# Attention value products of both weight parts in one 256-wide matmul, in a hybrid encoder block

## Chip, core and metric

The kernel runs on one core of one Trainium2 chip. The metric is the device time of one execution in microseconds (us). The kernel before has a median of 2099.49 us in three runs (2098.23 to 2099.73).

## Reference

One layer of an encoder in fp32 on 1024 tokens (16 rows of 64 columns) of width 1024. The change lies in the mixer, between the two feed-forward halves:

```python
u = rms_norm(h); q, k, v, s_in, gates = jnp.split(u @ w_in, splits, axis=-1)
# 8 heads of 64; a query sees min(8, rows) x 16 tokens around it, clamped at the grid's edge
sc = q . k * 64 ** -0.5 + bias          # in the window
pr = softmax(sc, axis=-1)
y_attn = (pr . v) @ w_attn_out
y_ssm = s5_branch(s_in, ...) @ w_ssm_out   # two-directional state scan, D skip, GLU
g_attn, g_ssm = sigmoid(gates)
h = h + (g_attn * y_attn + g_ssm * y_ssm) @ w_out
```

Before it stands `h + swiglu(rms_norm(h)) / 2`; behind it another such half, a small per-layer embedding with a gate, and a last norm.

## The kernel before

**Number format.** TensorE (PE) reads fp32 values that are split in two: a high part, which ScalarE (ACT) rounds into the format that PE takes (`split`, L152 to L154, a CAST), and a low part, the rest, which VectorE (DVE) subtracts out. A product of two split operands is three matmuls (`mm3`, L182 to L186: high by high, high by low, low by high), most of them 512 wide.

**Order of work.** The order of PE's instructions is the order of the code, written by hand. DVE, ACT, GpSimd (POOL) and SyncE (SP, which issues most loads) are put in order by a scheduler when the kernel is built, but for the start and `end()` (L1678), whose DVE and ACT order is the code's too. An engine runs its instructions strictly in that order. Tiles come out of rings of a fixed number of buffers: a writer waits until the last reader of the buffer's earlier content is done. The rings that matter: `x`, 56 buffers of 128 x 512 (`thid` and `tx`); in the mixer `w`, 12 of 128 x 1024 (`tw`: weights split in high and low, keys, and so on); `st`, 3 of 128 x 1024 for raw loads; `tmp`, 4 of 128 x 512; and 8 banks of PSUM (`bank`).

**Stages.** First feed-forward half to about 700 us, mixer to about 1255 us, its output product, second feed-forward half, embedding, last norm to 2094.5 us. In the mixer PE works through projections of `u` (24 matmuls, 512 wide, per output tile of 128 x 512: q, k, v, the state branch's input, 16 gate tiles). A generator, `mixer_side` (L1286), runs beside it: `tick()` after each three matmuls of a projection counts down, and when the count is up the next piece of the generator is issued in the middle of the projection. So the attention and the state branch are small insertions between 512-wide matmuls.

**Attention** comes in 64 units j: 8 heads, 2 row halves, 4 column blocks. A unit has 128 queries and 12 x 24 or 12 x 32 keys. At iteration j of the generator (one each 4 ticks, each 3 ticks from j = 48):

- `attn_scores` (L1198): two matmuls, 288 or 384 wide (L1207, L1208), then bias, maximum, exponential and division on DVE and ACT; the weights stay in `sm`.
- `attn_turn` (L1219) for unit j - 3: three transposes by PE (L1223) into a bank `pt`, split by ACT (L1226) into `pth` and by DVE (L1227) into `ptl`.
- `attn_values` (L1230) for unit j - 5: the values `vhl` of 64 dimensions lie high beside low, 128 columns. For each of three key groups one matmul of `pth`, 128 wide, with all 128 columns as weights (L1235: rows 0 to 63 get v_high x p_high, rows 64 to 127 v_low x p_high), and one of `ptl` with the 64 high columns (L1237, added to rows 0 to 63). A bank `O` collects four column blocks; after the fourth ACT copies the lower rows out (L1241), DVE adds them to the upper rows and brings the columns into token order (L1242), and a DMA from ACT's queue stores 64 x 512 in `o_d` (L1245).
- two steps of the state scan on POOL (L1092 to L1094, tile `X`), 128 steps in all; at j = 48 all that are left.

From j = 48 each iteration also takes one of 16 pairs of state groups: `ssm_out` (L1097) loads coefficients (`emi`), copies the pair's states out of `X` into `xs` by two ACT and two DVE copies (L1111), and three iterations later PE forms `yo` from them (L1117, L1119); ACT copies `yo` out (L1121).

After the units comes the state branch's GLU. Then `load_br` (L1400) loads both branches, the attention from `o_d` as two loads of 128 x 1024 per row half, and splits them into `bh` and `bl` for the products `br`.

Of the kernel before, what the change touches and what calls it, by code (L numbers as in the profile page):

```python
# [8 lines left out]
F32 = mybir.dt.float32  # L9
# [7 lines left out]
P = 128  # L17
SEQ = 1024
HT = 512
# [19 lines left out]
def encoder_block(ctx, tc, I, out):  # L39
# [73 lines left out]
    a2_d = dtile("a2_d", [NF // 2, 7, P, HT])  # L113
    h2_d = dtile("h2_d", [P, NK * SEQ])
    v_d = dtile("v_d", [SEQ, 512])
    o_d = dtile("o_d", [512, SEQ])
    g_d = dtile("g_d", [16, P, SEQ])
    y_d = dtile("y_d", [NPD, P, NCH])
    y2_d = dtile("y2_d", [512, SEQ])
# [81 lines left out]

        return tc.issue_after(mark["ins"]) if "ins" in mark else nullcontext()

    def rstd(m, r, q):
        A.activation(r, m, AF.Abs_reciprocal_sqrt, bias=eps)
        V.tensor_tensor(q, r, r, ALU.mult)
        V.scalar_tensor_tensor(q, m, eps, q, ALU.add, ALU.mult)
        V.scalar_tensor_tensor(r, q, -3.0, r, ALU.add, ALU.mult)

    class Norm:  # L210
# [33 lines left out]
        def stat(self, r=None, summed=False):  # L244
            if summed:
                m = self.acc
            else:
                m = bank("ms")[:, 0:self.n]
                sums = [self.acc] + self.more
                for i, sq in enumerate(sums):  # L250
                    T.matmul(m, lhsT=ones, rhs=sq, start=i == 0, stop=i == len(sums) - 1)
            q = tmq("rq", [P, self.n])
            r = thid("rs", [P, self.n], F32) if r is None else r
            rstd(m, r, q)
            self.r = r

        def apply(self, gi, res, every):
# [839 lines left out]
    def ssm_out(pr):  # L1097

        ms = []
        for g in range(2):  # L1100
            em = thid("emi", [P, 4, NCH], F32)
            nc.sync.dma_start(em[:, 0:3].rearrange("p a b -> p (a b)"), e_d[2 * pr + g])
            nc.sync.dma_start(em[:, 3], u_d[2 * pr + g])
            ms.append(em)

        xs = tw("xs", [P, 2, 2, NCH], F32)
        for g in range(2):
            for r in range(2):
                s0 = Xv[g * 64:(g + 1) * 64, r, pr, 0:1]
                both = bass.AP(tensor=s0.tensor, offset=s0.offset, ap=[list(s0.ap[0]), [NCH + 2, 2], [1, NCH]])  # L1110
                (A.copy if g == r else V.tensor_copy)(xs[r * 64:(r + 1) * 64, g], both)  # L1111

        def go():
            o = bank("yo")
            for g in range(2):
                oo = o[:, g * NCH:(g + 1) * NCH]
                T.matmul(oo, lhsT=ms[g][:, 0], rhs=ms[g][:, 3], start=True, stop=False)  # L1117
                for d in range(2):
                    T.matmul(oo, lhsT=ms[g][:, 1 + d], rhs=xs[:, g, d], start=False, stop=(d == 1))  # L1119
            ys = tmp("ys", [P, 2, NCH])  # L1120
            A.copy(ys, o[:, 0:2 * NCH].rearrange("p (g c) -> p g c", g=2))  # L1121
            nc.scalar.dma_start(y_d[2 * pr:2 * pr + 2].rearrange("g p c -> p g c"), ys)
        return go
# [10 lines left out]
    def qk_proj(hp, wq, wk):  # L1134
        qs, kh, kl = [], [], []
        for t in range(2):
            o = proj(wq, t, "q")
            for i in range(2):
                if t == 0:
                    qs.append(tw("qs"))  # L1140
                src = o[i * 64:(i + 1) * 64].rearrange("p (r b c) -> p r b c", r=8, b=4)
                hs, ls = slice(i * 64, (i + 1) * 64), slice((1 - i) * 64, (2 - i) * 64)

                def view(sl):
                    return qs[i][sl, hsl(t)].rearrange("p (b r c) -> p r b c", b=4, r=8)
                A.copy(view(hs), src)
                V.tensor_tensor(view(ls), src, view(hs).bitcast(F32), ALU.subtract)
        for t in range(2):
            o = proj(wk, t, "k")
            for i in range(2):  # L1150
                if t == 0:
                    kh.append(tw("kh"))
                    kl.append(tw("kl"))
                hs, ls = slice(i * 64, (i + 1) * 64), slice((1 - i) * 64, (2 - i) * 64)
                A.activation(kh[i][hs, hsl(t)], o[hs], AF.Copy, scale=0.125)
                A.activation(kh[i][ls, hsl(t)], o[hs], AF.Copy, scale=0.125)
                for s_ in (hs, ls):
                    V.scalar_tensor_tensor(kl[i][s_, hsl(t)], o[hs], 0.125, kh[i][hs, hsl(t)].bitcast(F32),
                                           ALU.mult, ALU.subtract)
        for i in range(2):  # L1160
            qkv[2 * hp + i] = (qs[i], kh[i], kl[i])

    def load_v(hd, cb):
        n = 4 * KNC[cb]
# [33 lines left out]
    def attn_scores(hd, rb, cb):  # L1198
        q, kh, kl = qkv[hd]
        n = KNC[cb]  # L1200
        nk = 12 * n
        qv = q[:, rb * HT + cb * P:rb * HT + (cb + 1) * P]
# [4 lines left out]
        T.matmul(s3, lhsT=qv, rhs=kv(kh), start=True, stop=False)  # L1207
        T.matmul(s3, lhsT=qv, rhs=kv(kl), start=False, stop=True)  # L1208
        sm = thid("sm", [P, 384], F32)[:, 0:nk]
        st = ap_.tile([P, 4], F32, tag="stat", bufs=4, name="stat")  # L1210
        V.tensor_tensor_reduce(out=sm.rearrange("p (r c) -> p r c", c=n), in0=s3,
                               in1=tabs[hd, rb][KVAR[cb]][:, :, 0:n], scale=-1.0, scalar=3.0e38,
                               op0=ALU.add, op1=ALU.min, accum_out=st[:, 0:1])
        A.activation(sm, sm, AF.Exp, bias=st[:, 0:1], scale=-1.0, accum_out=st[:, 1:2])
        V.reciprocal(st[:, 2:3], st[:, 1:2])
        A.activation(sm, sm, AF.Copy, scale=st[:, 2:3])
        return sm

    def attn_turn(cb, sm):  # L1219
        kp = 4 * KNC[cb]  # L1220
        tp = bank("pt")
        for g in range(3):
            T.transpose(tp[0:kp, ksl(g)], sm[:, g * kp:(g + 1) * kp], ident)  # L1223
# [6 lines left out]
    def attn_values(hd, rb, cb, O, ph, pl):  # L1230
        kp = 4 * KNC[cb]
        hl = vld[hd, cb]
        for g in range(3):

            T.matmul(O[:, ksl(cb)], lhsT=hl[0:kp, rb + g].rearrange("p h d -> p (h d)"), rhs=ph[0:kp, ksl(g)], start=(g == 0), stop=False,  # L1235
                     skip_group_check=True)
            T.matmul(O[0:64, ksl(cb)], lhsT=hl[0:kp, rb + g, 0], rhs=pl[0:kp, ksl(g)], start=False, stop=(g == 2),  # L1237
                     skip_group_check=True)
        if cb == 3:
            ot, ol = tmp("ot"), tmp("ol")  # L1240
            A.copy(ol[0:64], O[64:128])  # L1241
            V.tensor_tensor(ot[0:64].rearrange("p (r b c) -> p b r c", r=8, b=4),  # L1242
                            O[0:64].rearrange("p (b r c) -> p b r c", b=4, r=8),
                            ol[0:64].rearrange("p (b r c) -> p b r c", b=4, r=8), ALU.add)
            nc.scalar.dma_start(o_d[hd * 64:(hd + 1) * 64, hsl(rb)], ot[0:64])  # L1245


    ydr = y_d.rearrange("g (t o) c -> g o t c", o=16)
# [37 lines left out]
    def mixer_side():  # L1286
# [31 lines left out]
        for j in range(n + 6):  # L1318
            if j < n:
# [3 lines left out]
                if cb == 0 and j > 0:  # L1323
                    make_tabs(hd, rb)
                sms[j] = attn_scores(hd, rb, cb)
            if 0 <= j - 3 < n:
                pts[j - 3] = attn_turn(units[j - 3][2], sms.pop(j - 3))
            if 0 <= j - 5 < n:
                hd, rb, cb = units[j - 5]
                if cb == 0:  # L1330
                    O[hd, rb] = bank("O")
                attn_values(hd, rb, cb, O[hd, rb], *pts.pop(j - 5))
                if rb == 1 and hd + 1 < NH:
                    load_v(hd + 1, cb)
            scan_steps(2)
            if j >= SO:
                p = j - SO
# [62 lines left out]
    def load_br(t, b):  # L1400

        res = []
        if b == 0:
            for k in range(0, 4, 2):
                st = tst("br")
                nc.sync.dma_start(st.rearrange("p (k c) -> p k c", k=2),
                                  o_d[k * P:(k + 2) * P, hsl(t)].rearrange("(k p) c -> p k c", p=P))
                for i in range(2):
                    hi, lo = tx("bh"), tx("bl")
                    split(hi, lo, st[:, hsl(i)])  # L1410
                    res.append((hi, lo))
            return res
        for k in range(4):
# [264 lines left out]
    def end():  # L1678
# [131 lines left out]
```

## Time and profile before

| | before |
|---|---|
| median of 3 runs | 2099.49 us (2098.23 to 2099.73) |
| the profiled execution's time | 2096.29 us |
| its span in the profile | 2094.5 us |
| granted TensorE clock | 0.998 |
| busy: PE | 2074.5 us, 99% |
| busy: DVE, ACT, POOL | 1416.1 us (68%), 999.6 us (48%), 399.4 us (19%) |
| PE's value products | 192 of L1235, 192 of L1237 |

The profiled execution lies 3.2 us below the median of the runs, and 1.8 us of its time lie outside the span. In rows of the profile "L1235 PE MATMUL O<-pth,vhl" is a matmul at line 1235 that writes tile `O` from `pth` and `vhl`. Matmuls are pipelined: a row's start is good, its duration overlaps the next row, so that the price of a matmul is the distance from its start to the next start. An arrow behind a bracket names what ended the idle time before the row.

### The profile page before, as it was taken

How to read it: one execution, taken by the hardware profiler on the slowest of the kernel's cores; microseconds unless marked ns; L12 is line 12 of the kernel's file. 1: busy time of each engine (PE TensorE's matmuls, PEld its weight loads, DVE VectorE, ACT ScalarE, POOL GpSimd, SP SyncE). 2: the span in 40 equal slices, each digit the busy share in tenths (PEclk: the TensorE clock that was granted, in tenths of full speed). 3: DMA queues.
4: the chain of work that ended last, by engine and by line, in shares of the span. 5: the costliest groups of instructions: out<-in, count | busy, mean ns of one | idle time of the engine just before them, and what ended most of it. 6: DMA issues, size and time to landing. Idle time of an engine off the chain costs nothing.

```text
span 2094.5 us, 28063 instructions
## 1 busy us (share of the span) xinstructions
PE 2074.5 (99%) x9662; PEld 1705.4 (81%) x9662; DVE 1416.1 (68%) x2420; ACT 999.6 (48%) x1832; POOL 399.4 (19%) x636
## 2 busy tenths in 40 slices
PE   8999999999999999999999999999999999999998
PEld 3788888888888888888898888788888888888886
DVE  7897776667967334677753668995665665786855
ACT  6434333334445333667774635643333334445543
POOL 0037556441000006888200001000000000000000
PEclk9999999999999999999999999999999999999999
DMA  3435444475533551233477745243324238433302
GB/s 134 143 118 154 125 135 120 144 270 169 188 114 111 159 189 64 70 97 98 123 208 260 247 145 117 77 150 121 100 86 135 82 121 297 155 106 94 118 21 81
DMA packets 197744, 285.19 MB, mean 136 GB/s; under 512 B 41569, under 2 KB 81121, under 8 KB 197601
## 3 DMA queue, kind: packets, MB, share of 16 engines
q1 hardware_dynamic: 180304, 258.20, 38.8%
q10 hardware_dynamic: 14992, 21.00, 3.0%
q0 software_dynamic: 2304, 4.20, 1.2%
q8 instruction: 76, 1.25, 0.2%
q14 instruction: 68, 0.55, 0.1%
HBM read 201.01 MB, written 82.31 MB: 135 GB/s over the span
## 4 chain that ended last, share of the span: by engine, by line
PE 94%; DVE 2%; ACT 1%; DMA 1%; SPq 0%; issue 0%; DVEq 0%; ACTq 0%
PE dx L184 4%; PE dx L185 4%; PE dx L186 4%; PE gx L184 3%; PE ux L184 3%; PE ux L186 3%; PE gx L186 3%; PE gx L185 3%; PE ux L185 3%; PE gt L184 3%; PE gt L185 3%; PE gt L186 3%; PE dy L186 2%; PE dy L184 2%; PE dy L185 2%; PE gy L184 2%
## 5 line engine op out<-in xcount | busy, mean ns | idle before, releaser
L153 ACT CAST wh<-hbuf 128x512 fp32r<-128x512 f32 x280 | 173.0, 622 | 392.3 <-PE gx L185 80.9
L154 DVE TENSOR_TENSOR wl<-hbuf,wh 128x512 fp32r<-128x512 f32 x280 | 209.2, 750 | 122.7 <-ACT wh L153 120.5
L153 ACT CAST wh<-wblk 128x512 fp32r<-128x512 f32 x190 | 118.0, 622 | 192.6 <-PE dx L185 83.2
L154 DVE TENSOR_TENSOR wl<-wblk,wh 128x512 fp32r<-128x512 f32 x190 | 130.6, 690 | 49.3 <-ACT wh L153 41.8
L184 PE MATMUL dx<-ah,wh 128*128 128x512 f32 x416 | 163.3, 393 | 0.3 <-DVE hbuf L688 0.3
L186 PE MATMUL dx<-ah,wl 128*128 128x512 f32 x416 | 161.9, 389 | 0.0
L185 PE MATMUL dx<-al,wh 128*128 128x512 f32 x416 | 161.8, 389 | 0.0
L1092 POOL TENSOR_TENSOR sc<-X,rho 128x128 f32<-128x128 f32 x128 | 77.9, 609 | 327.2 <-ACT X L1075 317.3
L154 DVE TENSOR_TENSOR al<-araw,ah 128x512 fp32r<-128x512 f32 x154 | 106.3, 694 | 50.1 <-PE dx L185 21.1
L184 PE MATMUL gx<-xh,wh 128*128 128x512 f32 x320 | 124.9, 390 | 1.2 <-DVE c L575 1.2
L184 PE MATMUL ux<-xh,wh 128*128 128x512 f32 x320 | 125.0, 390 | 0.0
L186 PE MATMUL ux<-xh,wl 128*128 128x512 f32 x320 | 124.5, 389 | 0.0
L185 PE MATMUL gx<-xl,wh 128*128 128x512 f32 x320 | 124.5, 389 | 0.0
L186 PE MATMUL gx<-xh,wl 128*128 128x512 f32 x320 | 124.5, 389 | 0.0
L185 PE MATMUL ux<-xl,wh 128*128 128x512 f32 x320 | 124.5, 389 | 0.0
L153 ACT CAST ah<-araw 128x512 fp32r<-128x512 f32 x154 | 94.9, 619 | 43.2 <-PE dx L185 12.6
L184 PE MATMUL gt<-xh,wh 128*128 128x512 f32 x256 | 102.7, 401 | 0.0
L186 PE MATMUL gt<-xh,wl 128*128 128x512 f32 x256 | 99.8, 390 | 0.0
L185 PE MATMUL gt<-xl,wh 128*128 128x512 f32 x256 | 99.8, 390 | 0.0
L422 DVE TENSOR_TENSOR hbuf<-hbuf 128x512 f32<-128x512 f32 x120 | 91.4, 762 | 2.1
L184 PEld LDWEIGHTS dx<-ah,wh 128*128 128x128 f32 x416 | 78.1, 188 | 17.8 <-issue 0.7
L185 PEld LDWEIGHTS dx<-al,wh 128*128 128x128 f32 x416 | 78.1, 188 | 16.9 <-issue 0.7
(381 smaller groups left out, 5590.2 us busy)
## 6 DMA issues: line engine op xcount, KB each, us to landing
araw<-a_d SPq DMA_DIRECT2D x154, 256.0 KB
a_d<-c SPq DMA_DIRECT2D x148, 256.0 KB
wblk<-in_wd SPq DMA_DIRECT2D x88, 256.0 KB
hbuf<-in_wg SPq DMA_DIRECT2D x40, 512.0 KB
hbuf<-in_wu SPq DMA_DIRECT2D x40, 512.0 KB
wst<-in_win SPq DMA_DIRECT2D x26, 512.0 KB
hbuf<-in_xT SPq DMA_DIRECT2D x32, 256.0 KB
h_d<-hbuf ACTq DMA_DIRECT2D x32, 256.0 KB
```

The lines of the kernel that those rows point to most:

```text
L153: A.copy(hi, src)
L154: return eng.tensor_tensor(lo, src, hi.bitcast(F32), ALU.subtract)
L184: T.matmul(o, lhsT=wh, rhs=xh, start=first, stop=False, skip_group_check=more)
L185: T.matmul(o, lhsT=wh, rhs=xl, start=False, stop=False, skip_group_check=more)
L186: T.matmul(o, lhsT=wl, rhs=xh, start=False, stop=last, skip_group_check=more)
L422: V.tensor_tensor(b11, (b12, b22, None, None, b21)[i - 2], b11, ALU.subtract)
L1092: G.tensor_tensor(sc, both, rho4, ALU.mult)
```

## The change

1. **Value products.** The high and low part of the turned weights go into one tile `ptb` (128 x 3 x 2 x 128, a ring of two of its own), so that for each key group both lie side by side. One matmul 256 wide with all 128 columns of `vhl` as weights takes the place of the two: three per unit, not six. A bank `O` now holds two column blocks, for each of them the products of both parts.
2. **Evacuation.** After each second block ACT copies the p_high half (128 x 256) into `ot` (a ring of two), DVE adds the v_high x p_low product to its upper 64 rows, and one DMA stores both row halves of `ot` in the two planes of `o_d`: 32 stores in place of 16, the columns left in block order.
3. **Order.** Within an iteration the values of unit j - 5 now come ahead of the turn of unit j - 3.
4. **Loading the branch.** `load_br` reads two planes per tile pair (four loads of 512 KB per row half, not two), DVE adds them (128 x 1024), and the columns are brought into token order by the split's access pattern.
5. **Rings.** `qs` (as half tiles) and `xs` come out of the large ring `x` and no longer out of `w`, which has 10 buffers in place of 12.
6. **Tail.** In `end()` the two activations `scaled(6)` and `scaled(7)` are issued right behind the last norm's square root rather than ahead of it.

```diff
-    o_d = dtile("o_d", [512, SEQ])
+    o_d = dtile("o_d", [2, 512, SEQ])
...
-    def rstd(m, r, q):
+    def rstd(m, r, q, mid=None):
         A.activation(r, m, AF.Abs_reciprocal_sqrt, bias=eps)
+        if mid is not None:
+            mid()
...
-    cur.update(st=(ap_, "st", 3), w=(ap_, "w", 12), tmp=(ap_, "tmp", 4))
+    cur.update(st=(ap_, "st", 3), w=(ap_, "w", 10), tmp=(ap_, "tmp", 4))
...
-        xs = tw("xs", [P, 2, 2, NCH], F32)
+        xs = thid("xs", [P, 2, 2, NCH], F32)
...
-                if t == 0:
-                    qs.append(tw("qs"))
+                q = thid("qs")
+                qs.append(q)
...
-        ph = thid("pth", [P, 384])
-        pl = thid("ptl", [P, 384])
-        A.copy(ph[0:kp], tp[0:kp, 0:384])
-        V.tensor_tensor(pl[0:kp], tp[0:kp, 0:384], ph[0:kp].bitcast(F32), ALU.subtract)
-        return ph, pl
+        pb = ap_.tile([P, 3, 2, P], F32R, tag="ptb", bufs=2, name="ptb")
+        src = tp[0:kp, 0:384].rearrange("p (g q) -> p g q", g=3)
+        A.copy(pb[0:kp, :, 0], src)
+        V.tensor_tensor(pb[0:kp, :, 1], src, pb[0:kp, :, 0].bitcast(F32), ALU.subtract)
+        return pb
...
+        o = O["o"][:, (cb % 2) * 256:(cb % 2) * 256 + 256]
         for g in range(3):
-            T.matmul(O[:, ksl(cb)], lhsT=hl[0:kp, rb + g].rearrange("p h d -> p (h d)"), rhs=ph[0:kp, ksl(g)], start=(g == 0), stop=False,
+            T.matmul(o, lhsT=hl[0:kp, rb + g].rearrange("p h d -> p (h d)"), rhs=pb[0:kp, g].rearrange("p h q -> p (h q)"), start=(g == 0), stop=(g == 2),
                      skip_group_check=True)
-            T.matmul(O[0:64, ksl(cb)], lhsT=hl[0:kp, rb + g, 0], rhs=pl[0:kp, ksl(g)], start=False, stop=(g == 2),
-                     skip_group_check=True)
-        if cb == 3:
-            ot, ol = tmp("ot"), tmp("ol")
-            A.copy(ol[0:64], O[64:128])
...
+        ot = ap_.tile([P, 256], F32, tag="ot", bufs=2, name="ot")
+        ov = ot.rearrange("p (b q) -> p b q", b=2)
+        src = O["o"].rearrange("p (b h q) -> p h b q", b=2, h=2)
+        A.copy(ov, src[:, 0])
+        V.tensor_tensor(ov[0:64], src[0:64, 1], ov[0:64], ALU.add)
+        nc.scalar.dma_start(o_d[:, hd * 64:(hd + 1) * 64, rb * HT + (cb - 1) * P:rb * HT + (cb + 1) * P], ot)
...
+                st = [tst("br") for _ in range(2)]
+                for w in range(2):
+                    nc.sync.dma_start(st[w].rearrange("p (k c) -> p k c", k=2),
+                                      o_d[w, k * P:(k + 2) * P, hsl(t)].rearrange("(k p) c -> p k c", p=P))
+                V.tensor_tensor(st[0], st[0], st[1], ALU.add)
...
-        scaled(6, six[3])
         added(a, b, s, hm)
         fin[2].square(7, V)
-        scaled(7, hm)
         finish(1, (4, 6))
-        fin[2].stat()
+        fin[2].stat(mid=lambda: (scaled(6, six[3]), scaled(7, hm)))
```

What this moves on the engines is seen at two places. First PE's row around one unit, here inside a gate tile `gt`, before:

```order
L186 MATMUL gt_9804<-xh_5813,wl_9417 128x512
L1207 MATMUL s_9814<-kh_8896,qs_8669 128x288
L1208 MATMUL s_9814<-kl_8897,qs_8669 128x288
L1223 MATMUL pt_9823<-ident_73,sm_9670 96x128 x3
L1235 MATMUL O_9745<-pth_9741,vhl_9642 128x128
L1237 MATMUL O_9745<-ptl_9742,vhl_9642 64x128
L1235 MATMUL O_9745<-pth_9741,vhl_9642 128x128
L1237 MATMUL O_9745<-ptl_9742,vhl_9642 64x128
L1235 MATMUL O_9745<-pth_9741,vhl_9642 128x128
L1237 MATMUL O_9745<-ptl_9742,vhl_9642 64x128
L184 MATMUL gt_9804<-xh_5856,wh_9416 128x512
```

And PE's row after, at a unit from j = 51 on, where the state outputs `yo` of an earlier pair stand behind it:

```order
L186 MATMUL gt_10073<-xh_6271,wl_9683 128x512
L1209 MATMUL s_10130<-kh_9592,qs_9492 128x288
L1210 MATMUL s_10130<-kl_9593,qs_9492 128x288
L1239 MATMUL O_10139<-ptb_10040,vhl_9902 128x256 x3
L1225 MATMUL pt_10143<-ident_73,sm_9965 96x128 x3
L1119 MATMUL yo_10161<-emi_9993 128x128
L1121 MATMUL yo_10161<-xs_9999,emi_9993 128x128 x2
L1119 MATMUL yo_10161<-emi_9996 128x128
L1121 MATMUL yo_10161<-xs_9999,emi_9996 128x128 x2
L184 MATMUL gt_10073<-xh_6280,wh_9682 128x512
```

Six value products have become three wide ones, and they stand ahead of the transposes. The second place is ACT's row where it copies the fifth pair's states, before (`sm` are attention weights, `gs` a gate tile on its way out):

```order
L1214 ACTIVATE sm_10098,stat_10099<-sm_10098,stat_10099 128x288
L1121 COPY ys_10149<-yo_10142 128x256
L1111 COPY xs_10137<-X_6140 64x256 x2
L1121 COPY ys_10203<-yo_10196 128x256
L1216 ACTIVATE sm_10098<-sm_10098,stat_10099 128x288
```

And ACT's row after, for the same pair, whose states are now `xs_9999`, the tile that the row of PE above reads:

```order
L1248 COPY ot_10089<-O_10032 128x256
L1228 CAST ptb_10097<-pt_10093 96x3x128
L1250 DMA o_d_81<-ot_10089 2x64x256
L1172 CAST vhl_9983<-vf_9978 96x4x64
L1123 COPY ys_10118<-yo_10111 128x256
L1124 DMA y_d_83<-ys_10118 128x2x128
L153 CAST wh_10555<-wst_10553 128x1024
L1113 COPY xs_9999<-X_6140 64x256 x2
L1228 CAST ptb_10147<-pt_10143 96x3x128
```

A cast of a whole weight tile now stands directly ahead of the copies. Its buffer, `wh_10555`, is the one in which the keys `kh_9592` lay, and these are read for the last time by the matmul `s_10130<-kh_9592` of PE's row above.

More of the change, by code (lines that the diff above doesn't have):

```diff
@@ L1201, in attn_scores @@
         nk = 12 * n
-        qv = q[:, rb * HT + cb * P:rb * HT + (cb + 1) * P]
+        qv = q[rb][:, ksl(cb)]
         def kv(kt):
@@ L1325, in mixer_side @@
                 sms[j] = attn_scores(hd, rb, cb)
+            if 0 <= j - 5 < n:
+                hd, rb, cb = units[j - 5]
+                if cb % 2 == 0:
+                    O.setdefault((hd, rb), {})["o"] = bank("O")
+                attn_values(hd, rb, cb, O[hd, rb], pts.pop(j - 5))
+                if rb == 1 and hd + 1 < NH:
+                    load_v(hd + 1, cb)
             if 0 <= j - 3 < n:
                 pts[j - 3] = attn_turn(units[j - 3][2], sms.pop(j - 3))
[L1328 to L1334, printed above, removed]
             scan_steps(2)
@@ L1404, in load_br @@
             for k in range(0, 4, 2):
-                st = tst("br")
-                nc.sync.dma_start(st.rearrange("p (k c) -> p k c", k=2),
-                                  o_d[k * P:(k + 2) * P, hsl(t)].rearrange("(k p) c -> p k c", p=P))
+                st = [tst("br") for _ in range(2)]
[3 more added lines that the diff above has]
+                V.tensor_tensor(st[0], st[0], st[1], ALU.add)
                 for i in range(2):
                     hi, lo = tx("bh"), tx("bl")
-                    split(hi, lo, st[:, hsl(i)])
+                    sv = st[0][:, hsl(i)].rearrange("p (b r c) -> p r b c", b=4, r=8)
+                    hv, lv = (x.rearrange("p (r b c) -> p r b c", b=4, r=8) for x in (hi, lo))
+                    split(hv, lv, sv)
                     res.append((hi, lo))
```

16 lines of the change are left out of this document (7 added, 9 removed).

## Prediction

> **What bounds the kernel now.** I read the page first, its engines and its chain, then PE's waits, then the timeline of PE around single units. The first lines of the page, and of its chain:
>
> ```profile
> span 2094.5 us, 28063 instructions
> PE 2074.5 (99%) x9662; PEld 1705.4 (81%) x9662; DVE 1416.1 (68%) x2420; ACT 999.6 (48%) x1832; POOL 399.4 (19%) x636
> PE 94%; DVE 2%; ACT 1%; DMA 1%; SPq 0%; issue 0%; DVEq 0%; ACTq 0%
> ```
>
> PE is busy for 99% of the span and carries 94% of the chain. What it waited for (us in total, times, longest), the longest and the two that the change can touch:
>
> ```profile
> PE g L651 <- ACT xg L336: 5.0, 1, 5.0
> PE yo L1117 <- DVE ot L1242: 0.7, 1, 0.7
> PE yo L1117 <- DMA emi<-u_d: 0.4, 1, 0.4
> ```
>
> In the stretch of the units PE waits for these two, about a microsecond. So every microsecond of PE's own work there counts in full, and only a wait that is new can give it back.
>
> **Part 1, the value products.** PE's timeline gives the price as the distance between starts. A unit without values (start, duration):
>
> ```profile
> 847.73 0.29 PE L1207 MATMUL s<-kh,qs 128*128 128x288 f32 x1
> 847.86 0.30 PE L1208 MATMUL s<-kl,qs 128*128 128x288 f32 x1
> 848.00 0.49 PE L1223 MATMUL pt<-ident,sm 128*128 128x128 f32 x3
> 848.24 0.48 PE L184 MATMUL gt<-xh,wh 128*128 128x512 f32 x1
> 848.56 0.39 PE L185 MATMUL gt<-xl,wh 128*128 128x512 f32 x1
> 848.79 0.39 PE L186 MATMUL gt<-xh,wl 128*128 128x512 f32 x1
> ```
>
> From the first score to the start of the second 512-wide matmul it is 0.83 us, and 0.23 of them belong to the first 512-wide one (848.56 to 848.79 is the distance of such a matmul): 0.60. A unit with values:
>
> ```profile
> 936.68 0.29 PE L1207 MATMUL s<-kh,qs 128*128 128x288 f32 x1
> ...
> 937.19 0.31 PE L1235 MATMUL O<-pth,vhl 128*128 128x128 f32 x1
> ...
> 937.68 0.23 PE L1237 MATMUL O<-ptl,vhl 128*64 128x128 f32 x1
> 937.74 0.45 PE L184 MATMUL k<-xh,wh 128*128 128x512 f32 x1
> 938.02 0.39 PE L185 MATMUL k<-xl,wh 128*128 128x512 f32 x1
> ```
>
> The same stretch: 938.02 - 936.68 - 0.23 = 1.11. The six products cost 1.11 - 0.60 = 0.51 us. A matmul 256 wide with 128 columns of weights isn't in the mixer, but in the embedding 24 stand in a row (first, second and the one behind the last):
>
> ```profile
> 2067.50 0.28 PE L184 MATMUL pg<-xh,whh 128*128 128x256 f32 x1
> 2067.61 0.28 PE L185 MATMUL pg<-xl,whh 128*128 128x256 f32 x1
> 2070.37 0.28 PE L184 MATMUL pp<-pph,whh 128*128 128x256 f32 x1
> ```
>
> 24 in 2.87 us is 0.120 each, three 0.36. So a unit saves 0.51 - 0.36 = 0.155 us, and 64 units 9.9 us. Bounds: not dearer than the 288-wide score (0.13 to 0.14 in the unit above: 3 x 0.13 = 0.39, saving 7.7), not cheaper than half of a 512-wide one (0.115: 0.345, saving 10.6). I take 9.9, from the rows of the very width.
>
> The Trainium skill, "TensorE: Matmul & The Clock Gate", section "Back-to-back issue gap", gives a sustained distance of about 81 ns at width 128 and 131 ns at 512; an estimate between them is 97 ns at 256, hence 6 x 81 = 486 ns before, 291 after, and 12.5 us saved. The row above has 0.23 us where the page has 131 ns; by the trace the figure doesn't hold here.
>
> **Parts 2 and 3, evacuation and order.** Groups of the mixer (line, engine, form, count, then busy time and mean ns), and the stores' issue (ns, least, median, most):
>
> ```profile
> L1241 ACT COPY ol<-O 64x512 f32<-64x512 f32 x16 | 9.3, 584 | 1.8 <-PE yo L1119 1.5
> L1242 DVE TENSOR_TENSOR ot<-O,ol 64x512 f32<-64x512 f32 x16 | 10.9, 680 | 4.3 <-ACT ol L1241 4.2
> L1121 ACT COPY ys<-yo 128x256 f32<-128x256 f32 x16 | 5.9, 366 | 3.2 <-PE yo L1119 1.8 <-DMA y_d<-ys 1.2
> L1245 ACTq DMA_DIRECT2D o_d<-ot x16: 452/453/507, 865.9 to 1108.3; - x16
> ```
>
> ACT's 16 copies of 0.58 us become 32 of 0.37 (as `ys`, also 128 x 256): +2.5 us over 270 us. DVE's 16 adds of 0.68 become 32 of 0.34 to 0.42, from nothing to +2.6. Sixteen more stores add 16 x 0.45 us of issue on ACT's queue, 7.2 us over the 242 us from the first to the last of before. DVE is busy for 68% and ACT for 48% of the span, and the values use weights that were turned two iterations before: 0. A bank `O` is given back after two units, so that more banks are turned over; the 0.7 us at `yo` behind `ot` should go, and the wait for `emi` (0.4) grow by about as much, since its load has less of PE's work to hide behind: together 0, bounds -0.7 to +0.7. Without that cover each late `ot` would cost its 0.7.
>
> **Part 4, the branch's load.** The casts of the first half's attention, two of its state branch, whose split has a strided pattern, and the first product that reads them:
>
> ```profile
> 1138.85 2.56 ACT L153 CAST bh<-br 128x512 fp32r<-128x512 f32 x4
> ...
> 1159.19 2.14 ACT L153 CAST bh<-br 128x512 fp32r<-128x512 f32 x2 [1.12 <-DVE sg L1281]
> L184 PE MATMUL br<-bh,wh x6: 389/389/389, 1168.0 to 1171.4; 128*128 128x512 f32 x6
> ```
>
> The first four end at 1141.4, the product starts at 1168.0: 26 us of cover. Added per row half: two adds on DVE of about 1.2 us (128 x 1024, the `wl` row below), two loads of 512 KB on SP's queue, and splits with a strided pattern too: 1.07 rather than 0.64 us each, 4 x 0.43 = 1.7 us more on ACT, and I take as much for DVE. The weight loads queued behind them on SP start later by as much. All of it is under 10 us against 26: 0. If the cover were gone, the price would be these 10.
>
> **Part 5, the rings.** Here the order shows a new wait. A whole weight cast, `wh_10555`, stands ahead of the copies into `xs_9999` on ACT; it can't start before the last reader of its buffer, PE's first score matmul of a unit, is done, and `yo` behind the same unit needs `xs_9999`. What such things last is in the trace of before (weight cast, a weight split that waits for a score, four copies, and PE from that score to `yo`):
>
> ```profile
> 1082.14 1.05 ACT L153 CAST wh<-wst 128x1024 fp32r<-128x1024 f32 x1
> 1084.13 1.22 DVE L154 TENSOR_TENSOR wl<-wst,wh 128x1024 fp32r<-128x1024 f32 x1 [1.61 <-PE s L1207]
> 1015.26 1.64 ACT L1111 COPY xs<-X 64x256 f32<-64x256 f32 x4
> 1083.73 0.29 PE L1207 MATMUL s<-kh,qs 128*128 128x288 f32 x1
> ...
> 1084.79 0.44 PE L1117 MATMUL yo<-emi 128*128 128x128 f32 x2
> 1085.06 0.61 PE L1119 MATMUL yo<-xs,emi 128*128 128x128 f32 x4
> ```
>
> The DVE split started 0.40 us after the score that released it. So, counted from the score: cast from 0.40 to 1.45, first copy done at 1.45 + 0.41 = 1.86. PE gets to its first `xs` product after 0.27 (scores) + 0.36 (values) + 0.24 (transposes) + about 0.11 (one `emi` product) = 0.98. It stalls 0.88, and the second copy adds little: +0.9 us. In the same place of the others of the 16 pairs no cast stands between, and their copies come several microseconds ahead. Bounds 0 (the buffer comes free elsewhere) to 2.0 (the second copy and ACT's work behind it are late too).
>
> **Part 6, the tail.** ACT's rows, the DVE row that reads them, and PE's sum (`ms`) that the root is taken of:
>
> ```profile
> 2084.57 0.89 ACT L1655 ACTIVATE hbuf<-hbuf,gains 128x256 f32<-128x256 f32 x2
> 2085.37 0.45 ACT L205 ACTIVATE rs<-ms,eps 128x256 f32<-128x256 f32 x1
> 2085.85 0.42 DVE L206 TENSOR_TENSOR rq<-rs 128x256 f32<-128x256 f32 x1
> 2084.60 0.70 PE L251 MATMUL ms<-sq,ones 128*128 128x256 f32 x2 [0.70 <-DVE sq L232]
> ```
>
> DVE starts at 2085.85, when `rs` is done at 2085.82. PE's sum is there at 2085.30, so the square root gains at most 0.07: 0.
>
> **Sum.** 2096.3 (the profiled execution) - 9.9 + 0.9 = 2087.3. That execution lies 3.2 under the median, so for the median 2099.5 - 9.0 = **2090.5 us**. With the bounds alone: 2099.5 - 10.6 - 0.7 = 2088.2 to 2099.5 - 7.7 + 0.7 + 2.0 = 2094.5.
>
> **Rivals.** *A: the cast ahead of the copies is the rule.* If a weight cast or another late ACT instruction holds the copies at all 16 pairs, 16 x 0.9 = 14.4 us come in against 9.9: 2099.5 + 4.5 = 2104.0, slower. It decides from 9.9 / 16 = 0.62 us a pair. For it: four copies take 1.64 us, and the ring that they are written to now serves many others. Against: the order shows one place of the kind. 7%; and 10% that several new waits of this kind together (5 to 9 us) eat most of it: 2095.5 to 2099.5, no change.
>
> *B: the scan isn't faster.* Its last row, and its last three multiplications (ns, least, median, most), to set beside the first `xs` copy above at 1015.26:
>
> ```profile
> 1009.87 0.39 POOL L1094 TENSOR_TENSOR X<-sc,X 128x64 f32<-128x64 f32 x1
> L1092 POOL TENSOR_TENSOR sc<-X,rho x3: 517/518/714, 1005.5 to 1008.9; 128x128 f32<-128x128 f32 x3
> ```
>
> `X` is final at 1010.26, 5.0 us ahead of the copies. By j = 48, 43 units' values have saved 6.7 us, so copies that kept their place would wait up to 1.7. PE needs them only some 10 us later, hence 0 in the sum. But ACT and DVE stand still behind them. The same multiplication takes 0.52 or 0.71 us; if in the denser stretch every second of the 128 steps were of the slow kind that is fast now, the scan would end 64 x 0.2 = 12.8 us later, 14.5 after the copies' place, and PE would wait 4.5: 2095.0. 4%. The Trainium skill, "SBUF — State Buffer", section "Who interferes with whom", has a port pair that GpSimd and a VectorE instruction with two SBUF inputs lock against each other; the two durations agree with that, but these rows don't show what ran on DVE beside them.
>
> *C: the wide product does not save.* If 256 columns of this kind cost two 128-wide ones with full weights (2 x 0.11), three cost 0.67, not 0.51: +10 us, 2110.4. The 24 rows of 0.120 speak against it: 2%.
>
> *D: more is saved.* The wide products go at the lower bound (0.345), both old waits at `yo` (0.7 + 0.4) go, and the new one does not come: 2099.5 - 10.6 - 1.1 = 2087.8. 6%. By the figures of the page on TensorE in the Trainium skill it would be 2099.5 - 12.5 + 0.9 = 2087.9.
>
> **How the numbers follow.** Forecast 71%, 2088.2 to 2094.5; A 7% and its part 10%; B 4%; C 2%; D 6%. The range leaves out A, C and half of A's part: 2087.2 to 2097.0. A measurement of this kernel can tell about 0.2%, 4.2 us: faster means under 2095.3. Faster: forecast, D and B, 0.81; same: A's part, 0.10; slower: A and C, 0.09.
>
> **What would show it.** Right: PE's busy time near 2065; three rows of L1239 0.12 apart; one wait of 0.7 to 1.2 us at a `yo` product (L1121) for ACT's `xs`, behind a cast `wh`; nothing waited for at `br`. Wrong: O products 0.2 apart (C), waits at L1121 that add up to 5 us or more (A), POOL's last row later than 1010.5 with ACT idle behind it (B).

## The result, and the profile after

The changed kernel takes 2118.64 us (median of 5 runs, 2116.03 to 2125.61), the kernel before 2099.49 (5 runs, 2098.23 to 2099.92): a ratio of 1.0098 [1.0087, 1.0109]. The forecast was 2090.5 in a range of 2087.2 to 2097.0. The change is slower by 19 us where 9 fewer were forecast, and none of the rivals is what happened.

The first two lines of the page after:

```profile
span 2116.9 us, 27762 instructions
PE 2077.6 (98%) x9470; PEld 1703.2 (80%) x9470; DVE 1422.2 (67%) x2440; ACT 996.6 (47%) x1848; POOL 403.9 (19%) x636
```

The span grew by 22.4 us, from 2094.5. PE's idle time went from 2094.5 - 2074.5 = 20.0 to 39.3, and its busy time rose by 3.1 although it runs 192 matmuls fewer. So two things need a reason: 19.3 us of new waits, and busy time that should have fallen by 9.9.

First, whether part 1 did what it was priced at. PE's timeline around one unit with values (start, duration):

```profile
938.24 0.29 PE L1209 MATMUL s<-kh,qs 128*128 128x288 f32 x1
...
938.51 0.52 PE L1239 MATMUL O<-ptb,vhl 96*128 96x256 f32 x3
...
939.42 0.39 PE L185 MATMUL k<-xl,wh 128*128 128x512 f32 x1
```

Read as in the prediction, the unit takes 939.42 - 938.24 - 0.23 = 0.95 us against 1.11: 0.16 saved, where 0.155 was forecast. The loss is elsewhere. PE's waits from 800 to 1260 us (us in total, times, longest):

```profile
PE yo L1119 <- DMA emi<-u_d: 11.5, 6, 5.7
PE br L184 <- ACT bh L153: 2.9, 1, 2.9
PE O L1239 <- DVE ptb L1229: 1.3, 1, 1.3
PE yo L1119 <- DVE ptb L1229: 1.1, 1, 1.1
PE pt L1225 <- DVE stat L1213: 1.0, 2, 0.7
```

The first row stood at 0.4, once, before. It is a load: `u_d` into `emi`, 64 KB that SP issues. The longest of its six waits, in PE's timeline:

```profile
1047.99 0.49 PE L1225 MATMUL pt<-ident,sm 128*96 128x128 f32 x3
1054.20 0.77 PE L1119 MATMUL yo<-emi 128*128 128x128 f32 x2 [5.73 <-DMA emi<-u_d]
...
1057.51 0.63 PE L185 MATMUL gt<-xl,wh 128*128 128x512 f32 x1
1057.94 0.63 PE L186 MATMUL gt<-xh,wl 128*128 128x512 f32 x1
```

Behind the wait two 512-wide matmuls start 0.43 us apart, not 0.23 as elsewhere (each row lasts 0.63 us, not 0.39), and the windows there show why (stretch, us, busy us of PE, PEld, DVE, ACT, POOL, then granted clock, DMA share, GB/s):

```profile
1053.00:1054.00 1.00, 0.00 (x0) 0.00 (x0) 0.96 (x4) 0.48 (x2) 0.00 (x0) 0.50 0.14 47
...
1058.00:1059.00 1.00, 1.00 (x4) 0.81 (x3) 0.00 (x0) 0.96 (x4) 0.00 (x0) 0.50 0.68 139
```

From 1053 to 1059 PE was granted half its clock. The Trainium skill, "TensorE: Matmul & The Clock Gate", Part 1, has the array at half clock after an idle window of about 3.4 us and back at full after a busy one of that length. This trace agrees roughly, with 5.73 us of waiting and full clock again by 1060, behind some 5 us of work. A shorter wait can be enough: in `planes`, an experiment told below, PE waits 2.33 us before 1045.05, and the granted clock is 0.50 from 1045 to 1048. There the measurement decides. So a wait of a few microseconds can be paid twice.

Now why the load was late. SP's timeline and, below it, a store of ACT's queue:

```profile
1047.68 0.32 SPq L1105 DMA_DIRECT2D emi<-u_d  x1
...
1048.99 0.47 SPq L1105 DMA_DIRECT2D emi<-u_d  x1
1049.88 0.32 SPq L1104 DMA_DIRECT2D emi<-e_d  x1
1055.36 0.32 SPq L1105 DMA_DIRECT2D emi<-u_d  x1
```

```profile
1046.39 0.50 ACTq L1250 DMA_DIRECT2D o_d<-ot  x1
```

The load that PE waited for was already under way. PE goes on at 1054.20, and SP issues nothing between 1050.20 and 1055.36; by its place in the row it is the load of 1047.68, the fifth pair's `emi_9993`, which `yo_10161` reads in PE's row of the section on the change. The trace keeps an event for each part of a DMA that has landed. This load has 16 of them: 14 came within 3.7 us of the issue, the last two after 6.40 and 6.44 us, at 1054.12. The store of 1046.39 has one event at once and two at the end, the last at 1055.35. The engines in between (1052 to 1056, 40 slices of 0.1 us: busy tenths of the 16 engines; then packets, MB and share of SP's queue q1 and ACT's q10):

```profile
DMA  7852211111101111111110111111111111000000
q1 hardware_dynamic: 156, 0.17, 11.6%
q10 hardware_dynamic: 99, 0.08, 5.9%
```

From 1052.5 on about two engines are busy, and what is left of SP's loads moves there beside the store. All 32 two-plane stores have these two late events, and the loads of `emi` show what they cost: 31 were issued while such a store was under way and took 5.8 us in the median to their last event, the other 33 took 3.1. In `planes` both kinds take about 3.2. Of PE's six waits for `emi`, five, 11.3 of the 11.5 us, ended with a load that had been issued beside a store and took 5.2 to 6.4 us.

There is a second way from the store to the loads. SP stands still from 1050.20 to 1055.36, and what it waits for is written in the program: the `emi` load of the next pair and the store of `ot_10089` count their completion on the same one of eight counters, and each DMA of the two queues waits until the counter's last user has landed:

```order
L1105 DMA emi_10043<-u_d_76 128x128 [waits DMAHW4_49]
```

```order
L1250 DMA o_d_81<-ot_10089 2x64x256 [waits DMAHW4_49,DVE_49]
```

The load doesn't read what the store writes. It only takes its turn behind it, and SP's queue is in order, so that all later loads stand behind it too. This one was still in time, for its `yo` starts at 1061.10; of the six waits only the shortest, 0.2 us, ended with a load that SP had held back in this way. SP's waits from 1010 to 1112 us, after and then before:

```profile
SPq L1105 <- DMA o_d<-ot: 13.0, 3, 5.1
SPq L1169 <- DMA o_d<-ot: 12.0, 4, 3.5
```

```profile
SPq L1167 <- DMA o_d<-ot: 0.8, 1, 0.8
```

Such counters were shared before too, and it cost 0.8 us (another row has 0.3). What is new is how long the store is under way. One store of 128 KB alone on the DMA engines, after (941 to 946, 40 slices of 0.125 us) and, from an experiment told below, the same 128 KB with 128 rows outermost (`heads`, 942.5 to 944.5, slices of 0.05 us): GB/s by slice, packets, and share of the 16 engines:

```profile
GB/s 0 0 0 0 0 0 33 16 16 41 49 49 49 49 49 41 8 49 25 33 16 8 49 49 49 49 49 49 49 49 49 49 25 0 0 0 0 0 0 0
DMA packets 130, 0.13 MB, mean 26 GB/s; under 512 B 2, under 2 KB 130, under 8 KB 130
```

```profile
GB/s 0 0 0 0 0 0 0 0 0 0 0 0 0 0 0 0 0 0 0 0 164 246 389 430 389 348 369 205 62 21 0 0 0 0 0 0 0 0 0 0
DMA packets 144, 0.13 MB, mean 66 GB/s; under 512 B 16, under 2 KB 144, under 8 KB 144
```

The two-plane store moves for 27 slices, 3.4 us, never above 49 GB/s; the other for 10 slices, 0.5 us, at up to 430. Beside its 128 data packets it has 2 small ones, the other 16. Its access pattern begins with the two planes (2 x 64 x 256). The Trainium skill, "DMA: Bandwidth & Descriptors", "Why a DMA increments its semaphore by 16 and not by 1", says that a DMA runs on the largest number of engines up to 16 that divides the slowest dimension of both sides, and that each engine then posts one completion; 2 and 16 small packets agree with that to the unit, as do the two late events of each store and the share of 0.14 x 16 = 2.2 engines in the windows above.

### The profile page after: what moved, and what is told of

Same layout as the page of the kernel before. It is cut to its first block, busy times and chain, and to the rows that moved or that the text cites. A ratio compares the mean times of both kernels' runs of the same rounds, so it can differ in the third digit from the quotient of the medians.

```text
span 2116.9 us, 27762 instructions
## 1 busy us (share of the span) xinstructions
PE 2077.6 (98%) x9470; PEld 1703.2 (80%) x9470; DVE 1422.2 (67%) x2440; ACT 996.6 (47%) x1848; POOL 403.9 (19%) x636
## 4 chain that ended last, share of the span: by engine, by line
PE 42%; DMA 6%; DVE 3%; ACT 2%; issue 1%; SPq 0%; ACTq 0%; DVEq 0%
PE dx L184 2%; PE dx L186 2%; PE dx L185 2%; PE ux L185 2%; PE gx L185 2%; PE gx L186 2%; PE ux L186 2%; PE ux L184 2%; PE gx L184 2%; DMA o_d<-ot 1%; PE br L185 1%; PE br L186 1%; PE br L184 1%; PE dy L184 1%; PE dy L186 1%; PE dy L185 1%
```

## The experiments

The letters in the expectations stand for these theories. *L*: SP's loads wait for the completion of the `o_d` stores, because there are more of them (32, not 16) or because each is under way for longer. *W*, formed last and on record from `planes` on: it is the two-plane form, on about 2 engines. *B*: more traffic makes every load land later. *S*: the loads stand too late in SP's row. *R*: the new rings. *E* or *N*: the new casts and evacuation are slower by themselves. *P*: PE's faster units outrun what feeds them.

**Where the store is issued, and how many there are.** `store_pool` gives the same stores to GpSimd's queue; `store_16` gathers a row half in one tile and stores 256 KB once, still over two planes:

```diff
-        nc.scalar.dma_start(o_d[:, hd * 64:(hd + 1) * 64, rb * HT + (cb - 1) * P:rb * HT + (cb + 1) * P], ot)
+        nc.gpsimd.dma_start(o_d[:, hd * 64:(hd + 1) * 64, rb * HT + (cb - 1) * P:rb * HT + (cb + 1) * P], ot)
```

```diff
+        if cb == 3:
+            nc.scalar.dma_start(o_d[:, hd * 64:(hd + 1) * 64, hsl(rb)], ot)
```

> The changed kernel with the 32 stores of o_d issued from GpSimd's queue rather than ACT's, so that no load of SP's queue waits for their completion. Theory L (SP's loads of emi and vf wait, in the order of its row, for the completion of o_d stores, 25 us in the stretch of the state outputs, and so reach PE late): the waits of PE for emi go, 2090 to 2101 us. Theory R (the rings are the cause: emi and xs and qs share the large ring, and the small one has 10 buffers): the waits stay, 2112 us or more. Theory B (more traffic of the DMA engines makes each load land later): the bytes are the same, 2112 us or more.

> The changed kernel with one store per row half, 512 columns of both planes from one tile of the tmp ring: 16 stores rather than 32, the same bytes. Theory L: half of SP's waits for stores go, 2092 to 2104 us. Theories R and B: 2112 us or more.

`store_pool`: 2119.86, ratio 1.0101 [1.0086, 1.0116]. It settles little. No load of SP's row waits for `o_d` any more, and the stores still land 6.2 us after their issue in the median; but they now stand among the scan's steps in GpSimd's row, the last of which started at 1029.2 in place of 1013.8, so that another delay came in. `store_16`: 2136.81, 1.0181 [1.0165, 1.0196]. Half the stores cost 18 us more, which is the opposite of what a cost by number would do. SP's wait there and the store's transfer (944 to 953, slices of 0.225 us):

```profile
SPq L1169 <- DMA o_d<-ot: 13.4, 2, 8.3
```

```profile
GB/s 50 25 52 49 16 33 75 52 27 46 27 46 9 27 46 9 46 46 46 46 55 55 46 55 46 55 55 46 55 46 55 55 55 9 0 0 0 0 73 55
```

One store is under way for over 7 us and one wait lasts 8.3. Both runs came out where *R* and *B* had them, not *L*; *W* keeps of *L* only how long one store is under way.

**Loads on another queue, or earlier.** `emi_pool` issues the `emi` loads from GpSimd; `early_emi` issues them two iterations ahead of their products; `early_v` loads the values three iterations earlier; `early_both` does both; `gs_act` takes the stores of `g_d` out of SP's row:

```diff
-            nc.sync.dma_start(em[:, 3], u_d[2 * pr + g])
+            nc.gpsimd.dma_start(em[:, 3], u_d[2 * pr + g])
```

```diff
+            if 0 <= j - SO + AHEAD < NPAIR:
+                ems[j - SO + AHEAD] = ssm_load(j - SO + AHEAD)
```

```diff
+            if 0 <= j - 2 < n:
+                hd, rb, cb = units[j - 2]
```

```diff
-        nc.sync.dma_start(g_d[m, :, hsl(t)], gs)
+        nc.scalar.dma_start(g_d[m, :, hsl(t)], gs)
```

> The changed kernel with the loads of emi issued from GpSimd's queue, which is idle after the scan, so that they stand behind no wait of SP's row. Theory L: PE's waits for emi go, those for vf may stay, 2092 to 2106 us. Theory R: the loads still wait for their buffers in the large ring, 2112 us or more. Theory B: they land as late as now, 2112 us or more.

> The changed kernel with each pair's emi loads written two iterations earlier, the copies of the states and the products where they are. Theory S (loads stand in SP's row behind waits on work of the same or the next unit, so that emi, vf or both come late whichever one store is moved away): PE's waits for emi shrink, those through vf stay, 2098 to 2113 us. Theory E (the new evacuation and the ptb cast make ACT and DVE late, whatever the loads do): 2112 us or more.

> The changed kernel with the value loads vf written three iterations earlier, seven units ahead of their use rather than four. Theory S: ACT's waits for vf (12.7 us in the stretch of the state outputs) go, what waits for emi stays, 2098 to 2113 us. Theory E: 2112 us or more.

> Both: emi two and vf three iterations earlier. Theory S: few waits are left in the stretch, 2090 to 2103 us. Theory E: 2112 us or more.

> The changed kernel with the gate tiles' stores issued by ACT, which makes them, rather than by SP, which waits for ACT there. Theory S: one of the waits of SP's row goes, the others stay, 2100 to 2116 us. Theory E: ACT has more to issue, 2116 us or more.

Measured: 2115.09 (1.0073 [1.0056, 1.009]), 2117.05 (1.0089 [1.0074, 1.0105]), 2111.55 (1.0062 [1.0047, 1.0077]), 2110.86 (1.0057 [1.004, 1.0074]) and 2115.55 (1.0084 [1.0069, 1.0099]). Each takes off at most 8 of the 19 us. `emi_pool` missed *L*'s range. Of *S*'s four ranges only those of `early_v` and `gs_act` held; *E* had `early_emi` right, and `early_both` fell between the two. With `emi` out of SP's row ACT still waits for the values' load, and with both loads early SP still waits for the store; a row of each:

```profile
ACT vhl L1172 <- DMA vf<-v_d: 22.6, 5, 7.8
```

```profile
SPq L1103 <- DMA o_d<-ot: 15.4, 5, 4.4
```

So the loads' place isn't the cause (*S* falls as the whole explanation); it only sets how much of the delay reaches PE. In `emi_pool` SP waits only 0.9 us for `o_d` from 1005 to 1125 us, and the time is just 3.6 us better. The counter alone therefore doesn't explain the loss, though that run also moved the loads to another queue.

**Parts of the change put into the kernel before.** `rings_only` is the kernel before with part 5 alone. `before_32` is the kernel before with each of its stores cut into two of 64 x 256. `wide_alone` is the kernel before with part 1 and banks of two blocks, but with two tiles of turned weights in the large ring (two casts and two subtractions a unit), both sums formed by DVE, and the old stores, rings and branch load:

```diff
+            for w in range(2):
+                c0 = rb * HT + w * 256
+                nc.scalar.dma_start(o_d[hd * 64:(hd + 1) * 64, c0:c0 + 256], ot[0:64, w * 256:(w + 1) * 256])
```

```diff
+        for x, s in ((pa, src[:, 0:2]), (pb, src[:, 2:3])):
+            A.copy(x[0:kp, :, 0], s)
+            V.tensor_tensor(x[0:kp, :, 1], s, x[0:kp, :, 0].bitcast(F32), ALU.subtract)
```

> The kernel before with part 5 alone: qs as half tiles and xs in the large ring, the small ring with 10 buffers. Theory L: no effect of its own, 2097 to 2103 us. Theory R: emi comes late here too, 2106 us or more.

> The kernel before with each store of o_d cut in two of 64 x 256: 32 stores rather than 16, nothing else. Theory L (the number of stores is the cause): 2105 us or more. Theories P and N: 2097 to 2103 us.

> The kernel before with the wide products alone: three matmuls 256 wide, their operand in two tiles of the large ring, two blocks per bank, the sum of the parts formed at once by DVE, and rings, order, one store per row half and the branch's load as before. Theory P: TensorE is as fast as in the changed kernel, so the waits come here too, 2105 us or more. Theory N: the saving is kept, 2088 to 2098 us.

`rings_only`: 2100.05 (10 runs), 1.0004 [0.9995, 1.0013]; `before_32`: 2099.12 (10 runs), 1.0006 [0.9996, 1.0015]. Neither the rings nor 32 stores in place of 16 cost anything that can be told: *R* falls, and the number of stores with it. `wide_alone`: 2105.51, 1.004 [1.0026, 1.0053], slower too and within *P*'s range, but not by *P*'s waits: nothing is left of those for `emi`, and 0.6 us of ACT's for the values. PE waits for its own second subtraction:

```profile
PE O L1237 <- DVE ptb L1229: 8.3, 9, 2.1
```

That is the price of its split casts, which the change doesn't have. It shows that the wide products don't by themselves make the loads late, and can't show their saving.

**Pace.** `pad` adds to the changed kernel one dummy matmul of 352 columns to all units but the first two, whose result is overwritten (62 x 0.16 = 10 us, what part 1 saves); `slow_4` gives each iteration from j = 48 on four steps of the other work and not three:

```diff
+            T.matmul(tp[:, 0:352], lhsT=hl[0:kq, rb].rearrange("p h d -> p (h d)"),
+                     rhs=pb[0:kq].rearrange("p g h q -> p (g h q)")[:, 0:352], start=True, stop=True)
```

```diff
-            yield 4 if j < SO else 3
+            yield 4
```

> The changed kernel with one added matmul 352 wide per unit, whose result is overwritten: it gives TensorE back the 0.16 us that the unit saves. Theory P (pace: the stretch of the state outputs is paced by loads and by the rows of SP, ACT and DVE, so that TensorE's saving is turned into waits there, and these cost clock as well): with the old pace most waits go, 2098 to 2106 us. Theory N (the new evacuation, casts, stores and rings are slower than the old ones whatever the pace): 2116 to 2128 us.

> The changed kernel with four ticks per iteration from j = 48 on, as before that, rather than three, so that 0.68 us more of 512-wide matmuls stand between the units. Theory P: the waits in the stretch go, and what is lost is little cover for the GLU at its end: 2090 to 2104 us. Theory N: the same work is still late, 2110 us or more.

`pad`: 2124.28, 1.0125 [1.011, 1.014]; `slow_4`: 2114.12, 1.0077 [1.0062, 1.0092]. With the old pace back, the waits at `yo` stay, and the time gets worse by 5.6: *P* falls. Both runs came out where *N* had them; what rules *N* out is `planes` below, which leaves casts, evacuation and rings as they are. More work per iteration hides some of the delay, as the earlier loads did.

**The form of the store.** `planes` issues each store as two, one plane each, same bytes to the same place. `heads` keeps one store but lays `o_d` out by heads, so that it is 128 rows x 256, and reads the branch in twice as many loads of half the rows:

```diff
+        for w in range(2):
+            nc.scalar.dma_start(o_d[w, hd * 64:(hd + 1) * 64, rb * HT + (cb - 1) * P:rb * HT + (cb + 1) * P],
+                                ot[w * 64:(w + 1) * 64])
```

```diff
-    o_d = dtile("o_d", [2, 512, SEQ])
+    o_d = dtile("o_d", [NH * P, SEQ])
...
+        nc.scalar.dma_start(o_d[hd * P:(hd + 1) * P, rb * HT + (cb - 1) * P:rb * HT + (cb + 1) * P], ot)
```

> The changed kernel with each store of o_d issued as two, one per plane, 64 x 256 each, so that no store has the two planes as its outer dimension. Theory W (the two-plane store moves on about 2 of the 16 DMA engines, at 47 GB/s, and lands 4 to 9 us after its issue; loads of SP's row that wait for its completion, and the tiles behind them, come late): the waits go, 2088 to 2096 us. Theory N (casts, evacuation and rings are slower whatever the stores do): 2110 us or more; so also theory L, for which 64 stores are worse than 32.

> The changed kernel with o_d laid out by heads, both parts of a head in 128 rows that follow one another: one store of 128 x 256 with the rows as its outer dimension, 32 stores as in the changed kernel; the branch's load in twice as many pieces of 64 rows. Theory W: 2088 to 2097 us. Theories N and L: 2110 us or more.

`planes`: 2094.10 (11 runs), 0.9978 [0.9969, 0.9987]; `heads`: 2097.66 (11 runs), 0.9997 [0.9989, 1.0006]. With twice the stores, and not a byte or another instruction changed, `planes` takes 24.5 us off the changed kernel: *N* falls, so does the number of stores in *L*, and so does *B*, since the bytes are the same. SP's wait and PE's at `yo` there, each beside 13.0 and 11.5 after:

```profile
SPq L1105 <- DMA o_d<-ot: 1.7, 1, 1.7
```

```profile
PE yo L1119 <- DMA emi<-u_d: 3.7, 2, 2.3
```

`heads` gains 21.0 and ends 0.7 above *W*'s range. It has the single fast store of the slices above, so that it is the form and not the cutting in two; that it ends 3.6 above `planes` goes with a wait of PE for the branch's cast (4.8 us), whose loads had to be cut as well, and with a scan whose last step starts at 1019.5 (1011.9 in `planes`). That I haven't tested apart, and the profiled execution of `heads` (2100.84) lies 3.2 above its median.

`pad_planes` and `planes_half` ask both questions again with the slow store gone. The first is `pad` with `planes`; the second is `store_16` with its 256 KB stored plane by plane (64 x 512, 32 stores):

```diff
+        if cb == 3:
+            for w in range(2):
+                nc.scalar.dma_start(o_d[w, hd * 64:(hd + 1) * 64, hsl(rb)], ot[w * 64:(w + 1) * 64])
```

> The run pad (one added matmul 352 wide per unit) with the stores by planes. Theory W: the same as the run planes plus what 64 such matmuls cost TensorE, 64 x 0.16 = 10 us: 2098 to 2106 us. Theory P or N: 2112 us or more.

> The stores by planes, one per plane and row half (64 x 512, 32 stores, the tile from the ring tmp): the same store count as in the changed kernel and the same bytes as the run store_16, but no plane as outer dimension. Theory W: 2090 to 2097 us, against 2136.8 of store_16. Theory N: no better than 2110 us.

`pad_planes`: 2102.92 (10 runs), 1.0017 [1.0008, 1.0026], 8.8 above `planes`: now PE's work counts in full again, near the 10 that the dummies are worth. `planes_half`: 2093.80 (10 runs), 0.9978 [0.9969, 0.9988], against 2136.81 for the same tile and the same bytes over two planes: 43 us by the form of the store alone.

**The best version.** `planes_emi` is `planes` with the `emi` loads two iterations earlier, and `planes_both` has the values' load three iterations earlier too (the edits of `early_emi` and `early_v`).

> The stores by planes, and each pair's emi loads two iterations earlier. Theory W: with the stores quick, what is left of PE's waits in the stretch (3.7 us for emi in the run planes) is the distance from the load's issue to its use, and goes: 2088 to 2093 us. If that wait is not from the load's place: 2093 to 2096 us.

> As planes_emi, and vf three iterations earlier. Theory W: vf is no longer waited for on the path, so this adds nothing: 2088 to 2094 us.

`planes_emi`: 2091.07, 0.9967 [0.9955, 0.998]; `planes_both`: 2088.02 (5 runs), 0.995 [0.9938, 0.9963], 9.8 us under the 2097.84 of the kernel before measured beside it. It beats both kernels. The earlier values were expected to add nothing to `planes_emi` and took off another 3.1 us: PE's 3.1 us of waiting for DVE's copy of `xs` there are gone. Its page, and its row of 1020 to 1120 us beside that of before and of after, in this order:

```profile
span 2086.3 us, 27816 instructions
PE 2066.2 (99%) x9470; PEld 1696.7 (81%) x9470; DVE 1422.8 (68%) x2440; ACT 999.2 (48%) x1848; POOL 402.9 (19%) x636
```

```profile
1020.00:1120.00 100.00, 99.79 (x598) 88.62 (x597) 54.29 (x140) 70.91 (x159) 0.00 (x0) 1.00 0.76 233
```

```profile
1020.00:1120.00 100.00, 98.93 (x642) 87.92 (x642) 52.19 (x138) 69.73 (x156) 0.00 (x0) 1.00 0.70 205
```

```profile
1020.00:1120.00 100.00, 84.42 (x491) 73.37 (x490) 43.95 (x125) 55.01 (x137) 0.00 (x0) 0.93 0.57 158
```

The same 9470 matmuls take 2066.2 us of PE here and 2077.6 after, 11.4 more. The mean granted clock is 0.999 here and 0.994 after; 0.005 of 2116.9 is 10.6 us, about that difference. The idle time is 20.1 here and 39.3 after. Together 11.4 + 19.2 = 30.6, the whole difference of the two spans.

## Why the prediction was wrong

- **What bounds the kernel:** right. PE's work counts in full as long as nothing new is waited for (`pad_planes`: 8.8 of 10).
- **Part 1, -9.9:** right, in mechanism and size. 0.16 us a unit after, and 192 matmuls fewer bring PE's busy time from 2074.5 to 2066.2 in `planes_both` (-8.3), whose median is 9.8 under before. With the fast store alone (`planes`) it is 4.8. How much of the rest the earlier loads would have given to the kernel before wasn't run; PE waited only 0.4 for `emi` there.
- **Parts 2 and 3, 0 with bounds of 0.7 either way:** this step failed. It counted the stores (16 more, 7.2 us of issue on ACT's queue) and took their transfers as before. It never asked how long one store is under way, though its shape changed from 64 rows to two planes of 64 rows, nor what moves on the same engines meanwhile, nor who waits for its landing. The trace of before already had that wait, SP's 0.8 us for `o_d`. What the runs showed in its place: about 2 of 16 engines, 3.4 us of transfer or more, `emi` loads beside it that take 5.8 us and not 3.1, 25.0 us of waits in SP's row within 100 us, 11.5 us of PE's waits at `yo`, and the lower clock behind them; 24.5 us in all, by `planes` against after.
- **The wait for `emi`, to grow by at most 0.7:** it grew by 11.1. Even with the fast store 3.7 remain in `planes`, and go when the load is issued earlier (`planes_emi`, 2 to 3 us faster). So this term was too small even without the slow store: the 3.7 us fall to 1.0 when PE gets its old pace back (`pad_planes`), that is, the shorter units uncover the loads by more than the 0.7 allowed for.
- **Part 4, 0 under 26 us of cover:** right in itself, since neither `planes` nor `planes_both` has a wait at `br`. The cover came from loads in SP's row; where that row is late, the cover is gone: PE waits 2.9 us after for `bh`.
- **Part 5, +0.9:** not found. `rings_only` is within 0.1% of before, and `planes_both` waits 0.2 us for ACT's `xs` where 0.9 was forecast (`planes_emi` waits 3.1 for DVE's copy of `xs`, which goes when the values are loaded earlier). The order shows the cast ahead of the copies, but the order alone doesn't say that they are late.
- **Part 6, 0:** nothing speaks against it: the square root starts 0.07 us behind PE's sum before and 0.04 in `planes_both`. It wasn't run alone.
- **The rivals:** A is not what happened: PE has no wait of that kind. B is there in part, since the scan's last step starts at 1013.8 after, 3.9 later than before, but in `planes_both` it starts at 1013.9 too, and the gain is whole. C falls by the unit's timeline, and D is near what `planes_both` reaches (2088.02 against 2087.8), by another way. The side "slower" was held by two mechanisms on PE and ACT alone; no rival was about a transfer.

What stays open: how the loss divides between the loads that land late beside the store and the 25 us that SP stands behind its counter, since an earlier stand-still also sets when a later load is issued; and why `heads` ends above `planes`.

## What to carry to other kernels

Price a changed DMA by four things, not one: its issue, its time under way, what else moves on the same engines meanwhile, and who waits for its completion, which may be a load that never touches its data but takes the same counter in an in-order queue. Look at the outermost dimension of each access pattern: a small one there (two planes) can cost more than twice as many DMAs with the rows outermost. And when a load's cover is a few microseconds thin, a wait on the bounding engine can be paid again in its clock, here already a single one of 2.33 us.

## What the runs showed of the hardware

- A store of 128 KB as 2 x 64 x 256 moved at no more than 49 GB/s with 2 small packets; as 128 x 256 at up to 430 GB/s with 16. The issue of the latter is cheaper too: 0.33 us in the median, against 0.50 for the two planes; 64 x 256 takes 0.45 (`planes`) to 0.50 (`before_32`).
- A slow store on two engines holds up loads that use all 16: of a load issued 1.3 us behind it 14 parts landed within 3.7 us, the other two after 6.4. `emi` loads beside such a store took 5.8 us in the median, others 3.1.
- Sixteen more stores of 64 x 256 are free (`before_32`: 1.0006 [0.9996, 1.0015]), though each takes 0.50 us of ACT's queue.
- A wait of 5.73 us on PE is followed by some 5 us of work at half clock (1054.2 to 1059), in which 512-wide matmuls start 0.43 us apart and not 0.23; a wait of 2.33 us in `planes` by some 3 us (1045 to 1048).
